# A streaming-encoder block: the gated recurrence before the forgetting attention, its projections in the dense stage

## The chip, the cores and the metric

The kernel runs on one core of a Trainium2 chip. The metric is the device time of one execution in microseconds (us). A core has a matrix engine (TensorE, "PE" in the profile, with its weight loads as "PEld"), VectorE ("DVE"), ScalarE ("ACT"), GpSimd ("POOL"), and queues for transfers, mostly issued by SyncE ("SP") and some by POOL.

## The reference, cut to what matters

The block takes 1024 frames (T) of width 1024. After a normalisation, one input projection feeds three token mixers and their gates; the merged result goes through an output projection and a gated convolutional FFN.

```python
h = _rmsnorm(x, norm_mix_g)
z = h @ w_in
(hq, hf, hi, hg, fq, fk, fv, ff, mq, gate_logits) = jnp.split(z, pts, axis=-1)
y_a = _hgrn2_mixer(hq, hf, hi, hg, ...)   # 4 heads, state 128x128
y_b = _fox_mixer(fq, fk, fv, ff, ...)     # 8 heads x 64, causal
y_c = _memory_mixer(mq, mem_kv, ...)      # 4 heads x 128, 256 memory tokens
gates = jax.nn.sigmoid(gate_logits).reshape(B, T, 3, 1024)
merged = (gates[:, :, 0] * (y_a @ w_br_hgrn) + gates[:, :, 1] * (y_b @ w_br_fox)
          + gates[:, :, 2] * (y_c @ w_br_mem))
x = x + merged @ w_out
x = x + _conv_glu_ffn(_rmsnorm(x, norm_ffn_g), ffn_w_up, conv_w, conv_b, ffn_w_down)
```

The recurrence `_hgrn2_mixer` keeps a state S per head: `S_t = diag(f_t) S_{t-1} + (1 - f_t) i_t`, `o_t = S_t q_t`, with `f = lb + (1 - lb) sigmoid(hf)`, `silu(hq)`, and an output normalised and multiplied by `silu(hg)`. The forgetting attention `_fox_mixer` is causal attention with normalised q and k and a bias from cumulated log forget gates.

## The kernel before, in words

**Products.** Nearly every product is made of three matmuls of split operands (`mm3`, L114 to L116): high by high, high by low, low by high. The high half of an operand is a cast, usually on ACT (L120, names with h), the low half a subtraction on DVE (L128, names with l). A *chunk* is 128 output channels for all 1024 frames. Plainly done (`cm_chunk`, channel-major), a chunk is 48 matmuls of 512 columns. Values, queries and keys of the forgetting attention and the values of the recurrence are made *token-major* (`token_major`): a step is 128 frames by 256 channels, 24 matmuls of 256 columns.

**The dense stage** makes chunks in pairs by a scheme of seven block products instead of eight: a pair takes 84 matmuls of 512 columns, not 96. It needs sums of blocks of the operand (names T1 to T4, B21, ...), made once at the start, and sums of weight blocks, loaded as `rw`. The same scheme serves the FFN and the down projection, with their own sums.

**Order.** Before the change:

1. start: norms, the memory's keys and values (weights `gh`/`gl`), two gate chunks as cover;
2. dense stage, 7 pairs: 4 chunks of memory queries, 10 of gates. Gates go to DRAM (`gd`) as tanh;
3. memory attention, woven with `fox_values` and `fox_proj(0)` (token-major);
4. eight heads of forgetting attention, `fox_attn(p, i)`. Heads with i = 0 have the next `fox_proj` beside them, heads with i = 1 three gate chunks; `fox_prep` transposes and splits a pair's q and k; the last two heads have `hgrn_values` beside them, and one gate chunk;
5. the recurrence: `hgrn_prep(0)` alone (three chunks: f, q, g), then `hgrn_mix(h)` for four heads, the first three each woven with `hgrn_prep(h + 1)`, the fourth with six chunks of the projection of branch 1 (`branch(1)`), of which two more are held behind the last recurrence matmul;
6. branches 0 and 2, output projection (operand `mh`/`ml`), FFN, down projection.

**A head of the recurrence** has two halves of 512 frames. Each half starts with matmuls of `kt` and `qq` (L931, into `A`), runs six levels (H = 64, 32, ..., 2), makes the state update (kE, transposed at L990; L995) and the output (L1001, L1003), and is normalised and transposed (L1022) into `ya`. In a level, DVE subtracts (L948, L949), ACT takes the exponential of X (L950), POOL multiplies one half of X (L951) and DVE the other (L952), and PE multiplies (L961 for the two largest levels, L970 for the others); DVE puts the result into A (L972).

**What sets the order of instructions.** Python generators are woven: `weave` steps the one that is least far along by its count of steps. A scheduler then orders each engine's stream by priority and readiness as it models it; `ahead` raises a mixer's priority by 300, `issue_after` adds an order edge that binds on the same engine. PE, ACT, DVE, POOL and SP's transfers each run in the order so fixed, so an instruction that waits holds all behind it on its engine.

## Time and profile before

| what | value |
|---|---|
| median of 3 runs | 1764.36 us (1763.67 to 1765.61) |
| profiled execution | 1764.18 us |
| its span | 1762.4 us |
| busy: PE, DVE, ACT, POOL | 99%, 67%, 45%, 19% |
| DMA | 227.36 MB, mean 129 GB/s |
| memory attention with its cover | about 236 to 324 us |
| forgetting attention | about 324 to 677 us |
| recurrence, first to last matmul | 690 to 917 us |

A group of the profile is one line of code on one engine: busy time, mean duration (ns), idle time of the engine just before, and what released it. In the timeline each row starts with start and duration; matmuls overlap, so their pace is read from start to start. A bracket at the end gives the idle time ahead of the row and its releaser. PEclk is the clock granted to PE as a share of full speed.

### The profile page before, as it was taken

To read this page: it belongs to the slowest core of one execution; us is meant where nothing else is said; L and a number is where in the kernel's file an instruction comes from. 1 tells how busy PE (TensorE), PEld (TensorE's weight loads), DVE (VectorE), ACT (ScalarE), POOL (GpSimd) and SP (SyncE) were. 2 spreads that over 40 slices of the span, in tenths; PEclk is the share of its full clock that TensorE was granted. 3 is DMA by queue.
4 is the path that set the end of the run, shared out by engine and by line. 5 is a ranking of instruction groups with operands and counts; after the bars stand their busy time and mean duration, and the time that the engine had idled before them with its cause. 6 is when DMAs were issued, how large, how long until landed. Compare 5 with 4: busy or idle time off the path is not lost.

```text
span 1762.4 us, 24530 instructions
## 1 busy us (share of the span) xinstructions
PE 1736.2 (99%) x9069; PEld 1471.4 (83%) x9069; DVE 1185.8 (67%) x2181; ACT 786.7 (45%) x1318; POOL 334.7 (19%) x431
## 2 busy tenths in 40 slices
PE   8999999999999999999989999999999999999998
PEld 6778899989898997888878888788888888778887
DVE  7656445665756567778866755797777877674654
ACT  8633356545555554445331233543343443433332
POOL 1100032443424333334230000111111111100000
PEclk9999999999999999999999999999999999999999
DMA  9533232221212211001226452466454445494772
GB/s 361 178 119 105 83 128 73 76 95 60 91 47 85 84 46 52 25 31 56 77 78 216 153 200 80 136 188 163 139 160 133 119 128 152 144 362 145 238 269 84
DMA packets 83209, 227.36 MB, mean 129 GB/s; under 512 B 9600, under 2 KB 12424, under 8 KB 83088
## 3 DMA queue, kind: packets, MB, share of 16 engines
q1 hardware_dynamic: 65040, 161.29, 26.1%
q0 software_dynamic: 18048, 64.50, 12.6%
q8 instruction: 71, 1.16, 0.3%
q14 instruction: 50, 0.41, 0.1%
HBM read 180.88 MB, written 67.93 MB: 141 GB/s over the span
## 4 chain that ended last, share of the span: by engine, by line
PE 97%; ACT 1%; DVE 1%; DMA 0%; issue 0%; SPq 0%; POOL 0%; DVEq 0%; ACTq 0%
PE pp L115 21%; PE pp L116 21%; PE pp L114 21%; PE lg L115 4%; PE lg L116 4%; PE lg L114 4%; PE tr L114 2%; PE tr L115 2%; PE tr L116 2%; PE lg L970 2%; PE po L836 1%; PE lg L795 1%; PE lg L794 1%; PE po L835 1%; PE po L116 1%; PE po L114 1%
## 5 line engine op out<-in xcount | busy, mean ns | idle before, releaser
L115 PE MATMUL pp<-ul,wh 128*128 128x512 f32 x412 | 165.6, 402 | 0.0
L116 PE MATMUL pp<-uh,wl 128*128 128x512 f32 x412 | 165.4, 401 | 0.0
L114 PE MATMUL pp<-uh,wh 128*128 128x512 f32 x412 | 163.2, 396 | 1.5 <-DVE zt L888 1.5
L115 PE MATMUL pp<-wl,uh 128*128 128x256 f32 (+1 forms) x512 | 145.7, 285 | 0.0
L116 PE MATMUL pp<-wh,ul 128*128 128x256 f32 (+1 forms) x512 | 145.3, 284 | 0.0
L114 PE MATMUL pp<-wh,uh 128*128 128x256 f32 (+1 forms) x512 | 144.7, 284 | 0.0
L120 ACT CAST wh<-s 128x512 fp32r<-128x512 f32 x113 | 68.4, 619 | 152.8 <-PE pp L115 76.8
L120 ACT CAST wh<-raw 128x1024 fp32r<-128x1024 f32 (+2 forms) x76 | 67.5, 890 | 98.9 <-PE pp L115 86.9
L1250 POOL DMA_DIRECT2D rw<-in_w_up x44 | 24.1, 554 | 403.4 <-ACT sqs L1185 169.9
L114 PEld LDWEIGHTS pp<-wh,uh 128*128 128x128 f32 x512 | 96.4, 189 | 1.2
L116 PEld LDWEIGHTS pp<-wh,ul 128*128 128x128 f32 x512 | 96.5, 189 | 0.9
L115 PEld LDWEIGHTS pp<-wl,uh 128*128 128x128 f32 x512 | 96.4, 188 | 0.9
L120 ACT CAST dwh<-wr 128x1024 fp32r<-128x1024 f32 (+1 forms) x42 | 41.1, 980 | 124.6 <-PE tr L115 41.7
L120 ACT CAST wh<-rw 128x512 fp32r<-128x512 f32 x83 | 50.6, 619 | 101.2 <-PE pp L115 59.7
L114 PEld LDWEIGHTS pp<-uh,wh 128*128 128x128 f32 x412 | 78.4, 190 | 17.5 <-DVE zt L888 1.7
L115 PEld LDWEIGHTS pp<-ul,wh 128*128 128x128 f32 x412 | 77.9, 189 | 16.8
L116 PEld LDWEIGHTS pp<-uh,wl 128*128 128x128 f32 x412 | 77.9, 189 | 15.5
L128 DVE TENSOR_TENSOR wl<-raw,wh 128x1024 fp32r<-128x1024 f32 (+2 forms) x76 | 78.4, 1033 | 17.9 <-ACT wh L120 12.7
L128 DVE TENSOR_TENSOR wl<-s,wh 128x512 fp32r<-128x512 f32 x113 | 77.0, 683 | 8.9 <-ACT wh L120 8.9
L128 DVE TENSOR_TENSOR wl<-rw,wh 128x512 fp32r<-128x512 f32 x83 | 55.7, 686 | 29.5 <-PE pp L116 14.1
L951 POOL TENSOR_TENSOR X<-X,kt 128x256 f32<-128x256 f32 x48 | 50.4, 1057 | 124.5 <-ACT X L950 119.5
L128 DVE TENSOR_TENSOR dwl<-wr,dwh 128x1024 fp32r<-128x1024 f32 (+1 forms) x42 | 47.6, 1133 | 39.0 <-ACT dwh L120 39.0
(471 smaller groups left out, 5185.7 us busy)
## 6 DMA issues: line engine op xcount, KB each, us to landing
rw<-in_w_up POOLq DMA_DIRECT2D x44, 512.0 KB, 4.6
sd<-in_w_dn POOLq DMA_DIRECT2D x30, 512.0 KB, 5.9
br<-yd SPq DMA_DIRECT2D x30, 512.0 KB, 5.3
raw<-in_w_cm SPq DMA_DIRECT2D x26, 512.0 KB, 3.4
gd<-gt SPq DMA_DIRECT2D x48, 256.0 KB, 2.0
gt<-gd SPq DMA_DIRECT2D x48, 256.0 KB, 2.8
yd<-fc SPq DMA_DIRECT2D x44, 256.0 KB, 2.5
wr<-sd SPq DMA_DIRECT2D x20, 512.0 KB, 4.4
```

The source lines that it names most:

```text
L114: PE.matmul(ps, lh, rh, start=first, stop=False, skip_group_check=more)
L115: PE.matmul(ps, lh, rl, start=False, stop=False, skip_group_check=more)
L116: PE.matmul(ps, ll, rh, start=False, stop=last, skip_group_check=more)
L120: S.copy(out, in_)
L128: return (sub or V).tensor_sub(l, src, h.bitcast(F32))
L794: PE.matmul(ps[:, :w], qa[i][:, tsl], kh[i][:, s0:s0 + w], start=True, stop=False)
L795: fox_sets[p][3] = PE.matmul(ps[:, :w], qa[i][:, tsl], kl[i][:, s0:s0 + w], start=False, stop=True)
L835: PE.matmul(o, vhl[:, sb, :], ph[:, src], start=(sb == 0), stop=False)
L836: PE.matmul(o, vhl[:, sb, :], pl[:, src], start=False, stop=last)
L951: G.tensor_mul(Xk, Xk, Kv[:, :, 0, :])
L970: PE.matmul(o[:, b * 64:(b + 1) * 64], X[:, b * P:(b + 1) * P], Xq[:, b * bpb:(b + 1) * bpb, :], start=True, stop=True)
L1250: late["raw"] = G.dma_start(raw[:, 2 * i:2 * i + 2, :], src[:, 2 * i:2 * i + 2, :])
```

## The change

The recurrence moves ahead of the forgetting attention, right behind the memory attention. In parts:

- **Dense stage.** All twelve recurrence chunks (q, f, g of four heads) go through it, with the 4 memory queries and 6 gates: 22 chunks, 11 pairs. Their evacuation applies the tanh form there and stores to DRAM (`hd`); `hgrn_load` loads a head's three tiles on SP's queue.
- **Memory attention** is woven with `hgrn_values` (into `Vh`) and two gate chunks.
- **Recurrence.** The four heads are woven with token-major work: `fox_values` (its values go to DRAM, `vfd`), `fox_proj(0)` and `fox_proj(1)` (to DRAM, `zd`), 8 steps a head (9 with the last). `held` ties each such step on PE behind the mixer's matmul three steps back. The normalisation and transposes of a half (`finish`) are issued at the third level of the following half, and its result goes to DRAM (`yad`). At H = 64 and for kE the subtraction goes into the bias of ACT's exponential.
- **Forgetting attention.** `fox_proj(2)` stands alone behind the last recurrence matmul; then eight heads, whose q, k and values come from DRAM, with `fox_proj(3)` beside the first, two gate chunks beside each of the next six, six chunks of `branch(0)` beside the last. Two more chunks are held behind the last PV matmul.
- **After it**, `yc` (memory branch) is loaded on POOL's queue behind the last softmax product, `yb` on SP's; the branches run in the order 0, 2, 1.
- **Smaller.** At the start, the scaling of `xk` tiles (L542) is ordered behind the last cast of x. In the FFN's first units, the casts B21h and T4h are ordered behind the weight casts o5 and o7. The down projection's first block (`down_operands`) is loaded, cast and split within the FFN's last unit.

By the instruction lists, PE has 8661 matmuls instead of 8709: 5760 of 512 columns by 128 instead of 5808, all others alike. DVE has 2211 rows instead of 2178, ACT 1317 instead of 1199, POOL 430 as before, SP 521 transfers instead of 456 (203 of 128x1024 instead of 175, 266 of 128x512 instead of 234).

```diff
-NCOVER, NPAIR = 2, 10
-NFOX = [0, 3, 0, 3, 0, 3, 1]
-_dense = [12, 13, 14, 15] + [16 + 8 * br + j for br, j in ORDER[4:4 + NPAIR]]
+ORDER = [(br, j) for br in (0, 2, 1) for j in range(8)]
+NCOVER, NPAIR, NMEM = 2, 6, 2
+NFOX = [0, 2, 2, 2, 2, 2, 2, 0]
+_dense = [12, 13, 14, 15] + [16 + 8 * br + j for br, j in ORDER[4:4 + NPAIR]] + list(range(12))
...
+            if ch < 12:
+                what, h = divmod(ch, 4)
+                d = t if what == 1 else gate_tile()
+                S.activation(d, t, AF.Tanh, scale=0.5)
+                if what == 1:
+                    V.tensor_scalar(d, d, TMIN, c1[:, h:h + 1], ALU.max, ALU.mult)
+                else:
+                    V.scalar_tensor_tensor(out=d, in0=d, scalar=1.0, in1=t, op0=ALU.add, op1=ALU.mult)
+                SP.dma_start(hd[h, what][:, sl], d)
+                return
...
-                with tc.issue_after(late["square"].ins) if t > 3 else nullcontext():
+                with tc.issue_after(late["square" if t > 3 else "x_cast"].ins):
                     S.activation(xk[t], xk[t], AF.Copy, scale=col(C_GX + t))
...
+    def held(gen, lag=LAG):
+        while True:
+            at = state.get("at", [])
+            with tc.issue_after(at[-lag].ins) if len(at) >= lag else nullcontext():
+                try:
+                    next(gen)
+                except StopIteration:
+                    return
+            yield
...
-    weave((chain(fox_values(), fox_proj(0)), 25), (ahead(memory(), AHEAD), 4 * MEM_STEPS))
+    weave((chain(hgrn_values(), gates_early(NMEM)), 16 + 2 * NMEM), (ahead(memory(), AHEAD), 4 * MEM_STEPS))
...
+        for what, t in ((1, at), (0, qt), (2, gz)):
+            SP.dma_start(t, hd[h, what])
...
+                if H == 64:
+                    nr = ph.tile([P, 4], F32, tag="nr", name="nr", bufs=2)
+                    S.activation(nr, Gv[:, :, 0, H - 1], AF.Copy, scale=-1.0)
+                    for b in range(nb):
+                        S.activation(Xk[:, b, :], Gv[:, b, 0, :], AF.Exp, bias=Gv[:, b, 0, H - 1:H], scale=-1.0)
+                        S.activation(Xq[:, b, :], Gv[:, b, 1, :], AF.Exp, bias=nr[:, b:b + 1])
...
+                if li == 2 and "fin" in state:
+                    state.pop("fin")()
...
-            V.tensor_sub(kE[:, :nb, :], G3[:, :nb, P - 1:P].to_broadcast([P, nb, P]), G3[:, :nb, :])
-            S.activation(kE[:, :nb, :], kE[:, :nb, :], AF.Exp)
+            for b in range(nb):
+                S.activation(kE[:, b, :], G3[:, b, :], AF.Exp, bias=G3[:, b, P - 1:P], scale=-1.0)
...
-    run_all(hgrn_prep(0))
-    for h in range(3):
-        weave((ahead(hgrn_mix(h, ya), AHEAD), HGRN_STEPS), (hgrn_prep(h + 1), 6))
+    open_hgrn()
+    hgrn_load(0)
+    fill = chain(fox_values(), fox_proj(0), fox_proj(1))
+    for h in range(4):
+        weave((ahead(hgrn_mix(h), AHEAD), HGRN_STEPS), (held(islice(fill, 8 + (h == 3))), 8))
+    state.pop("fin")()
+    with tc.issue_after(state["last"].ins):
+        run_all(fox_proj(2))
...
+    for p in range(4):
+        for i in range(2 if p < 3 else 1):
+            if i:
+                fox_prep(p + 1, fox_sets[p][3])
+            count = NFOX[2 * p + i]
+            weave((ahead(fox_attn(p, i), AHEAD), FOX_STEPS),
+                  (held(gates_early(count) if p + i else fox_proj(3)), 2 * count if p + i else 8))
...
+    weave((ahead(fox_attn(3, 1), AHEAD), FOX_STEPS), (held(branch(0, yh, yl, range(6))), 12))
+    with tc.issue_after(late["pv"].ins):
+        run_all(branch(0, yh, yl, (6, 7)))
...
                 if after == "snap":
                     order.enter_context(tc.issue_after(late["split"].ins))
+                    order.enter_context(tc.issue_after(late["o7" if name == "T4" else "o5"].ins))
...
+    def down_operands():
+        raw = pw.tile([P, 4, HB], F32, tag="rw", name="rw", bufs=2)
+        G.dma_start(raw[:, 0:2, :], w_dn[:, 0, 0:2, :])
+        G.dma_start(raw[:, 2:4, :], yd[:, 0, 0:2, :])
+        ops = [operand(raw[:, i, :]) for i in (0, 2, 1, 3)]
+        late["down"] = [Blocks([ops[i + 2 * j][q] for j in range(2)]) for i in range(2) for q in range(2)]
```

How the order moves is seen at three places. The first is PE where the recurrence begins. Before, its first matmuls (L931, from `qq` and `kt`) stood among the matmuls of a chunk of 512 columns (`pp`, a projection):

```order
L114 MATMUL pp<-uh_81,wh 128x512
L115 MATMUL pp<-ul_82,wh 128x512
L116 MATMUL pp<-uh_81,wl 128x512
L114 MATMUL pp<-uh_83,wh 128x512
L115 MATMUL pp<-ul_84,wh 128x512
L931 MATMUL lg<-qq,kt 128x192 x4
L116 MATMUL pp<-uh_83,wl 128x512
L114 MATMUL pp<-uh_85,wh 128x512
L115 MATMUL pp<-ul_86,wh 128x512
```

After the change, the same matmuls (now L951) follow the last matmuls of the memory attention (`po` from `mph`, `mvh`, its values by its probabilities):

```order
L117 MATMUL pp<-uh_85,wl 128x512
L115 MATMUL po<-mph,mvh 128x512
L116 MATMUL po<-mpl,mvh 128x512
L117 MATMUL po<-mph,mvl 128x512
L115 MATMUL po<-mph,mvh 128x512
L116 MATMUL po<-mpl,mvh 128x512
L117 MATMUL po<-mph,mvl 128x512
L951 MATMUL lg<-qq,kt 128x192 x4
L115 MATMUL pp<-wh,uh_71 128x256
L116 MATMUL pp<-wl,uh_71 128x256
L117 MATMUL pp<-wh,ul_72 128x256
```

The last projection chunk of 512 columns now ends ahead of the memory attention's last products, and the token-major fill (256 columns) begins behind the recurrence's first matmuls.

The second place is SP's queue there, after the change. `ychd` and `ycld` store the memory attention's results, `hmf` and `rs` are the recurrence's constants, `ha`, `hq` and `hz` are head 0 (the tiles of `hd`, in two parts), `raw` is a weight of the fill:

```order
L733 DMA ychd<-ych 128x512
L140 DMA raw<-in_w_fqk 128x1024
L733 DMA ycld<-ycl 128x512
L901 DMA hmf<-in_hmask 128x448
L904 DMA rs<-in_mats 128x512
L915 DMA ha_3582<-hd 128x1024
L915 DMA ha_3843<-hd 128x1024
L915 DMA hq_3581<-hd 128x1024
L915 DMA hq_3842<-hd 128x1024
L915 DMA hz_3583<-hd 128x1024
L915 DMA hz_3844<-hd 128x1024
```

Before, `hmf` and `rs` were followed by weights alone, since `ha`, `hq` and `hz` were made on the chip by `hgrn_prep`. The tiles of the constants lie in memory that the memory attention used: `hmf` waits for its last logits, `rs` for the last matmuls but one of the `po` above, and `hq` for the last.

The third place is PE in the last half of the recurrence. Before, from the second level (L961) to the output (L1001, L1003) only the mixer's own matmuls stood there:

```order
L961 MATMUL lg<-X 64x64 x4
L970 MATMUL lg<-X 128x64 x4
L1022 MATMUL tr<-ident,o_9129 128x128
L990 MATMUL tr<-ident,kE 128x128 x3
L970 MATMUL lg<-X 128x64 x4
L1022 MATMUL tr<-ident,o_9129 128x128 x3
L995 MATMUL tr<-Vf,kT 128x128 x3
L970 MATMUL lg<-X 128x64 x4
L1001 MATMUL po<-Vf,A 128x128
L1003 MATMUL po<-St,qe 128x128
```

After the change (L961 is L990, L970 is L1001, L990 is L1024, L1022 is L1058), 38 fill matmuls stand between the second level and the next; these rows are the last of them and what follows:

```order
L115 MATMUL pp<-wh,uh_81 128x256
L116 MATMUL pp<-wl,uh_81 128x256
L1001 MATMUL lg<-X 128x64 x4
L117 MATMUL pp<-wh,ul_82 128x256
L115 MATMUL pp<-wh,uh_83 128x256
L1058 MATMUL tr<-ident,o_5575 128x128
L1024 MATMUL tr<-ident,kE 128x128
L1058 MATMUL tr<-ident,o_5575 128x128
L1001 MATMUL lg<-X 128x64 x4
L1058 MATMUL tr<-ident,o_5575 128x128 x2
L1024 MATMUL tr<-ident,kE 128x128 x2
L116 MATMUL pp<-wl,uh_83 128x256
```

Behind these rows stand 25 more fill matmuls before L1029 and the next level, and 24 before the output. Every half of the recurrence looks like this now, with 92 to 96 fill matmuls of 256 columns, where most halves had 72 of 512 before.

More of the change, by code (lines that the diff above doesn't have):

```diff
@@ L1092, in branch @@
                 yield
[L1094 to L1100 removed]
+    first_branch()
+    weave((ahead(fox_attn(3, 1), AHEAD), FOX_STEPS), (held(branch(0, yh, yl, range(6))), 12))
+    with tc.issue_after(late["pv"].ins):
+        run_all(branch(0, yh, yl, (6, 7)))
+    pf.release()
+    pq.release()
     py = tc.alloc_tile_pool(name="py", bufs=1, side="right", reuse_waits="tile")
@@ L1243, in sum_of, with unit @@
         return t
-    def unit(src, put, begun=None, before=None, after=None):
+    def unit(src, put, begun=None, before=None, after=None, ahead=None):
         raw = pw.tile([P, 4, HB], F32, tag="rw", name="rw", bufs=2)
```

248 lines of the change are left out of this document (132 added, 116 removed).

## The prediction

> **What bounds the kernel now.** I read the page from its top: busy shares, then the chain of work that ended last, then the busy time and granted clock of chosen stretches.
>
> ```profile
> span 1762.4 us, 24530 instructions
> PE 1736.2 (99%) x9069; PEld 1471.4 (83%) x9069; DVE 1185.8 (67%) x2181; ACT 786.7 (45%) x1318; POOL 334.7 (19%) x431
> PE 97%; ACT 1%; DVE 1%; DMA 0%; issue 0%; SPq 0%; POOL 0%; DVEq 0%; ACTq 0%
> ```
>
> TensorE (PE) is the bound almost everywhere: 1762.4 − 1736.2 leaves only 26.2 us of idle time. So there are two ways to gain: fewer matmul columns, and the few places where PE waits or runs at a lower clock. The stretches show those places (columns: from:to, length, then PE, PEld, DVE, ACT and POOL busy, then PEclk, DMA share, GB/s).
>
> ```profile
> 98.00:195.00 97.00, 97.00 (x420) 78.52 (x419) 50.16 (x80) 36.09 (x64) 4.18 (x8) 1.00 0.28 95
> 324.00:367.00 43.00, 43.00 (x311) 40.41 (x310) 30.14 (x82) 23.93 (x46) 23.10 (x27) 1.00 0.30 95
> 586.00:678.00 92.00, 89.77 (x639) 83.34 (x638) 55.18 (x188) 47.68 (x99) 25.25 (x39) 1.00 0.20 66
> 678.00:700.00 22.00, 21.80 (x92) 17.67 (x92) 18.16 (x34) 11.67 (x17) 12.94 (x9) 0.92 0.16 50
> 690.00:867.00 177.00, 177.00 (x1006) 150.32 (x1006) 147.22 (x292) 79.58 (x137) 67.20 (x61) 1.00 0.13 44
> 891.00:933.00 42.00, 36.48 (x213) 32.26 (x212) 28.68 (x60) 14.86 (x28) 13.78 (x16) 0.92 0.36 128
> 1113.00:1124.00 11.00, 8.40 (x47) 6.93 (x45) 6.18 (x12) 9.42 (x20) 3.28 (x4) 1.00 0.40 143
> 1539.00:1553.00 14.00, 11.82 (x43) 8.98 (x43) 12.53 (x14) 5.24 (x6) 2.14 (x4) 0.88 1.02 373
> ```
>
> Row by row: the steady dense stage, one forgetting-attention head with its cover, the end of that attention, the beginning of the recurrence, its first six halves, its uncovered tail, the entry of the FFN and the entry of the down projection. The dense row gives the price of a matmul of 512 columns: 97.00 / 420 = 0.231 us. In the recurrence PE is full, but DVE is busy 147.22 of 177 us (83%): there the second engine is not far behind.
>
> **The change, part by part.** All sums are against the profiled execution, 1764.18 us (its span plus 1.8), which lies 0.2 below the median shown, 1764.36.
>
> *Fewer matmuls.* The dense stage goes from 7 to 11 pairs of chunks. A pair costs 84 matmuls of 512 columns there and 2 x 48 elsewhere, so 4 x 12 = 48 are gone: 48 x 0.231 = **−11.1 us**. Can the dense stage carry recurrence chunks? A pair there takes 84 x 0.231 = 19.4 us of PE, and DVE is busy 50.16 / 97 of it, 10.0 us. The new evacuations add up to four gate products per pair:
>
> ```profile
> L896 DVE SCALAR_TENSOR_TENSOR hq<-hq,zt 128x512 f32<-128x512 f32 x7 | 5.0, 718 | 1.2 <-ACT hq L890 1.1
> ```
>
> 4 x 0.72 = 2.9 us, so 12.9 of 19.4: hidden by the matmuls of the next pair. The new stores and loads of the DRAM tiles (SP, 28 + 32 more of the two large shapes) lie in stretches with a DMA share of 0.13 to 0.30; I cost them at nothing except at the entry below.
>
> *The uncovered tail.* Before, nothing is left to weave beside the last half of the recurrence. The stretch 891 to 933 shows 42.00 − 36.48 = 5.5 us idle and 42 x 0.08 = 3.4 us lost to a clock of 0.92.
>
> ```profile
> 895.52 0.81 PE L931 MATMUL lg<-qq,kt 128*128 128x192 f32 x4
> ...
> 901.39 1.08 PE L970 MATMUL lg<-X 128*128 128x64 f32 x8
> 907.63 1.97 PE L970 MATMUL lg<-X 128*128 128x64 f32 x8 [4.55 <-POOL X L951]
> ...
> 917.32 0.39 PE L1003 MATMUL po<-St,qe 128*128 128x128 f32 x2
> ```
>
> In the new order that place has 38 fill matmuls of 256 columns (the order of PE above). A head's 192 fill matmuls are worth this much:
>
> ```profile
> 340.16 0.28 PE L114 MATMUL pp<-wh,uh 128*128 128x256 f32 x1
> 340.28 0.28 PE L115 MATMUL pp<-wl,uh 128*128 128x256 f32 x1
> ```
>
> 0.118 us from start to start (0.12 in the rows, 0.1175 as a mean over ten), so 38 give 4.5 us and close the 4.55. I take **−8.9**, the whole of it; what the thinner cover costs elsewhere is a term of its own.
>
> *Attention to recurrence.* The lone first projection after the attention is gone.
>
> ```profile
> 678.20 0.72 PE L114 MATMUL pp<-uh,wh 128*128 128x512 f32 x1 [1.51 <-DVE zt L888]
> ...
> 679.15 0.63 PE L116 MATMUL pp<-uh,wl 128*128 128x512 f32 x1
> ```
>
> The two stretches hold 2.2 + 0.2 us of idle and 22 x 0.08 = 1.8 of clock: **−4.2**. At the new end of the attention, two chunks of branch 0 are held behind the last PV, and the loads of yc and yb get those 2 x 24 x 0.231 = 11 us and the last steps of the attention as cover.
>
> *Start, FFN entry, down entry.*
>
> ```profile
> 23.96 1.14 ACT L542 ACTIVATE xk<-xk,cv 128x1024 f32<-128x1024 f32 x1
> ...
> 26.08 0.51 PE L114 MATMUL po<-uh,gh 128*128 128x512 f32 x1 [1.35 <-ACT gh L120]
> ...
> 27.34 0.50 PE L116 MATMUL po<-uh,gl 128*128 128x512 f32 x1 [0.53 <-DVE gl L128]
> ```
>
> The scaling ahead of the cast gh moves behind the last x cast, so gh is 1.1 us earlier, or more: of 1.35 + 0.53 I take **−1.5**.
>
> ```profile
> 1118.37 2.08 ACT B21h L120 x4
> 1120.45 2.08 ACT T4h L120 x4
> ...
> 1123.10 0.50 PE L114 MATMUL pp<-T3h,wh 128*128 128x512 f32 x1 [2.60 <-ACT wh L120]
> ...
> 1545.40 0.79 PE L115 MATMUL pp<-dbl,dwh 128*128 128x512 f32 x1 [1.53 <-DVE dbl L128]
> ```
>
> The casts B21h and T4h now stand behind the weight casts o5 and o7, 4.2 us of ACT less in front of the waiting wh: **−2.3** of 2.60, the rest for the low half of that weight, which comes next. At the down projection the first block is loaded and split a unit earlier; the stretch loses 2.2 idle + 14 x 0.12 = 3.9, of which I take **−3.4**.
>
> Gains: 11.1 + 8.9 + 4.2 + 1.5 + 2.3 + 3.4 = **31.4 us**.
>
> *New: the entry into the recurrence.* PE now goes straight from the last memory matmuls to the first recurrence matmul, and the fill stands behind that. On SP's queue the loads ha, ha, hq wait in order behind rs, which waits for the last memory matmuls but one. No trace shows this place; the nearest rows are the issue of a DMA and its landing.
>
> ```profile
> 1.17 0.42 SPq L209 DMA_DIRECT2D mt<-in_memT  x1
> ...
> raw<-in_w_cm SPq DMA_DIRECT2D x26, 512.0 KB, 3.4
> ```
>
> Four issues at 0.42, a landing at 3.4, and two elementwise steps of 0.6 (like the 0.7 of L896) make 6.3 us of PE idle; then a clock at half pace, as after 907.63 (1.97 us for what took 1.08) or at 679.15, some 1.7 us. I take **+8**. Below it, +4 if the waits of rs fall early; above, +11 with a landing two microseconds later and a longer slow stretch. The matmul that waits holds the whole fill behind it.
>
> [...] The rows speak against a plain threshold: 1.51 us of idle was followed by half pace at 679.15 (0.63 us for a matmul that takes 0.39 to 0.40 elsewhere), and 2.60 us at 1123.10 was not. [...]
>
> *New: a recurrence with thinner cover.* Two rows give PE's work of the mixer:
>
> ```profile
> L115 PE MATMUL pp<-ul,wh 128*128 128x512 f32 x154 | 62.3, 405 | 0.0
> ...
> L115 PE MATMUL pp<-yl,wh 128*128 128x512 f32 x20 | 8.0, 399 | 0.0
> ```
>
> In 690 to 867 there are 3 x 174 matmuls of 512 columns, 120.6 us; the other 56.4 are three heads' own work, 18.8 a head, 9.4 a half. With 96 fill matmuls (11.3) a half now takes PE 20.7 us, where it took 177 / 6 = 29.5. Can the chain over ACT, POOL, DVE and PE go at that pace? The uncovered half of before, from 895.52 to the last L1003 at 917.32 with its wait and low clock, took about 22.0 us: 8 x (22.0 − 20.7) = 10. The change takes subtractions off DVE (H = 64 and kE) and defers each half's end, so I take **+9**. Ends: 0 if it all overlaps, and +29 if the DVE work of the fill comes on top of 22 us (rival b).
>
> *New: recurrence to attention.* 22.7 us of fox_proj(2) cover the last normalise; then fox_prep(0) has eight transposes and their splits with 24 matmuls beside them: **+2** (0 to 5, by the 1.5 to 2.6 us that such entries cost above). The attention heads keep covers of 22.2 or 22.7 us; a head with 22.7 ran full in 324 to 367, DVE at 30.14 of 43: nothing.
>
> New costs: 8 + 9 + 2 = 19. Sum: 1764.2 − 31.4 + 19 = **1752**.
>
> **The rivals.**
>
> *(a) POOL beside a busy DVE slows the recurrence.* POOL's multiply is the step for which PE waited 4.55 us:
>
> ```profile
> 900.24 0.73 POOL L951 TENSOR_TENSOR X<-X,kt 128x256 f32<-128x256 f32 x1 [4.53 <-ACT X L950]
> 903.33 4.25 POOL L951 TENSOR_TENSOR X<-X,kt 128x256 f32<-128x256 f32 x2 [2.36 <-ACT X L950]
> ...
> L951 POOL TENSOR_TENSOR X<-X,kt 128x256 f32<-128x256 f32 x48 | 50.4, 1057 | 124.5 <-ACT X L950 119.5
> ```
>
> One alone takes 0.73 us, two in the crowded tail 4.25, and the mean is 1.057. The halves get shorter, so DVE gets denser, and each half has six such multiplies in a chain: if each takes 0.4 us more than in my 22 us, half of them on the path, a half takes 23.1: 8 x 1.1 = 9 more, **1761**. For it: the two rows. Against: most multiplies are issued well ahead of their matmuls, as the stretch 690 to 867 without idle shows.
>
> [...]
>
> *(b) Slower: DVE work of the fill stands in the recurrence's chain.* Before, the cover brought few DVE instructions that could not wait; now each projection also brings a sum, a product and weight splits:
>
> ```profile
> L732 DVE TENSOR_TENSOR z<-z,fr 128x1024 f32<-128x1024 f32 x7 | 9.7, 1385 | 0.7 <-POOL fr L133 0.7
> L730 DVE TENSOR_REDUCE fr<-fsq 128x16 f32<-128x1024 f32 x7 | 8.5, 1219 | 1.6 <-ACT fsq L729 1.6
> ```
>
> Two of each, and two weight splits of about 1.0 (the mean of L128 below), are 7.1 us for a head that carries fox_proj, 3.6 a half; the first two heads carry fox_values, with the splits alone, 1.0 a half. If this mean of 2.3 comes on top of the 22.0 us, a half takes 24.3: 8 x 3.6 = 29 instead of 9, **1772**. It decides from the point where 31.4 − 8 − 2 = 21.4 us are used up, 2.7 us a half above PE's 20.7, so at 23.4 us. For it: DVE is nearly the bound by its work alone. These groups of 690 to 897, seven halves, belong to the old cover and leave it:
>
> ```profile
> L128 DVE TENSOR_TENSOR wl<-raw,wh 128x512 fp32r<-128x512 f32 (+1 forms) x17 | 16.3, 957 | 0.3 <-ACT wh L120 0.2
> L888 DVE TENSOR_TENSOR zt<-pp,rx 128x512 f32<-128x512 f32 x20 | 13.7, 683 | 3.0 <-PE pp L116 2.8
> ...
> L896 DVE SCALAR_TENSOR_TENSOR hz<-hz,zt 128x512 f32<-128x512 f32 x8 | 6.8, 846 | 0.1
> ...
> L980 DVE TENSOR_TENSOR kE<-Gt 128x512 f32<-128x512 f32 (+1 forms) x7 | 4.9, 698 | 0.0
> ```
>
> With hq's 5.0 they are 41.8 / 7 = 6.0 a half; L980 is 0.7 more that goes. So 147.22 / 6 = 24.5 becomes 24.5 − 6.0 − 0.7 + 3.6 = 21.4 in the last two heads, less the subtractions of H = 64 and the branch work of that stretch: about PE's 20.7. Against: this is no more than the +9 holds already (21.8 a half), and the fill's work on DVE can wait, since its next step is due a whole block later.
>
> *(c) Everything overlaps.* The recurrence stays at PE's pace (+0), the entry costs +4, the next entry +2: 1764.2 − 31.4 + 6 = **1739**.
>
> *(d) The dense saving does not arrive*, since the four extra evacuations of a pair hold PSUM: then + 11, **1763**. Against it stands DVE at 12.9 of 19.4 us.
>
> **How the numbers follow.** My forecast has 0.52 (1745 to 1758, the entry between +4 and +11 and the recurrence a few us either way). (a) has 0.18, (b) 0.13, (c) 0.13, (d) 0.04. Predicted: **1752**. The range takes in (a), (c) and (d), and the lower part of (b): **1738 to 1769**; what is left out is the rest of (b), about 0.1, and a gain beyond (c), as much. About 0.2%, 3.5 us, is what a measurement of this kernel tells from no change. Faster by more (below 1760.8): the forecast, (c), and somewhat under half of (a), **0.74**; within: the rest of (a), (d), and the lower end of (b), **0.14**; slower (above 1767.9): **0.12**.
>
> **What would show it.** 5760 matmuls of 512 columns instead of 5808 and no idle in the dense stage: the first term. A first recurrence matmul (L951) with 4 to 11 us of idle before it and a DMA hq or ha as releaser: the entry. Starts of the recurrence's halves 21.8 us apart on average: +9; at 20.7, case (c); at 23.1 with idle PE released by POOL X, (a); at 24 or more with DVE over 95% busy, (b). A matmul L1001 without a wait of several us in the last half, no waits of 2.60 for wh after B21h and of 1.53 for dbl: the gains. It would be wrong if the attention heads, with their loads from DRAM and the held cover, showed idle that 324 to 367 does not have, since the sum has nothing for them.

## The result, and the profile after

The changed kernel takes **1810.11 us** (median of 4 runs, 1806.11 to 1810.72), the kernel before 1764.26 us. The ratio is 1.0254 (95% interval 1.0236 to 1.0272): 2.5% slower. The prediction, 1752 with a range of 1738 to 1769, was wrong in size and in sign. All medians, here and below, are of fast runs; one slow execution of e6, of 3522 us, is left out.

The page of the changed kernel: its span, the busy shares, and the chain that ended last.

```profile
span 1808.8 us, 24826 instructions
PE 1748.3 (97%) x9021; PEld 1474.3 (82%) x9021; DVE 1207.3 (67%) x2215; ACT 815.9 (45%) x1436; POOL 312.8 (17%) x431
PE 85%; DVE 6%; DMA 3%; ACT 3%; issue 2%; POOL 1%; SPq 0%; DVEq 0%; ACTq 0%; POOLq 0%
```

PE has 48 matmuls fewer, and yet is busy 12.1 us longer (a busy PE at a lower clock counts in full: at 0.50 the matmuls of 512 columns from 694.35 to 695.63 took 0.63 us each, at 1.00 behind 696.42 they took 0.39 to 0.40); its idle time went from 26.2 to 60.5 us. The chain ran over PE for 97% before and for 85% now. So the time is lost in large part to waits, and to the clock behind them.

Where? The first and last logits of the memory attention, a group of the tile `mkh`, before the change and after it (times are of first and last start):

```profile
L114 PE MATMUL lg<-mkh,mqh x32: 277/282/366, 236.1 to 307.3; 128*128 128x256 f32 x32
```

```profile
L115 PE MATMUL lg<-mkh,mqh x32: 276/283/365, 315.3 to 386.1; 128*128 128x256 f32 x32
```

Up to that point the changed kernel is 79.2 us later: four more dense pairs at 19.4 (77.6), and little else. From there to the last matmul of the last mixer (the recurrence's L1003 before, at 917.3; the PV matmul now, at 969.3) it takes 654 us where 681 were needed: 27 us less. But eight chunks of 48 matmuls, 8 x 11.1 = 89 us of PE's work, left that stretch (twelve of the recurrence out, four of gates in). **89 us of cover went out and only 27 came back as time.** Behind the mixers 5.6 us are saved. 79.2 − 27 − 5.6 is the 46 us.

The stretches of the changed kernel that answer to those in the prediction (columns as there):

```profile
28.00:240.00 212.00, 210.75 (x911) 169.90 (x911) 136.82 (x214) 105.88 (x176) 16.07 (x24) 1.00 0.42 144
399.00:421.00 22.00, 7.01 (x34) 6.47 (x33) 12.13 (x21) 13.25 (x26) 4.46 (x5) 0.61 0.67 246
505.00:533.00 28.00, 23.27 (x170) 22.21 (x171) 22.46 (x45) 17.17 (x39) 10.41 (x9) 0.88 0.28 81
627.00:660.00 33.00, 26.31 (x168) 24.14 (x168) 23.19 (x75) 17.41 (x37) 15.88 (x24) 0.84 0.24 79
680.00:700.00 20.00, 14.48 (x60) 11.29 (x59) 16.04 (x46) 10.00 (x19) 12.88 (x16) 0.74 0.12 46
757.00:777.00 20.00, 16.07 (x75) 12.73 (x74) 15.43 (x42) 12.00 (x25) 10.70 (x18) 0.86 0.16 57
839.00:860.00 21.00, 17.07 (x81) 13.86 (x80) 16.22 (x49) 13.48 (x28) 11.35 (x20) 0.84 0.14 44
1165.00:1190.00 25.00, 23.41 (x118) 19.45 (x117) 22.01 (x41) 16.16 (x30) 6.61 (x9) 1.00 0.59 168
1580.00:1605.00 25.00, 25.00 (x110) 20.29 (x109) 20.02 (x24) 12.60 (x15) 4.22 (x8) 1.00 0.74 254
```

In order: the dense stage, full, so that its gain is real; the entry into the recurrence, with 15.0 us idle; the worst half of the recurrence; the beginning of the attention; the three joints of the attention, where the next pair's `fox_prep` runs; the FFN entry and the down entry. Counting idle time and clock together (length minus busy, plus length times the missing share of the clock), the beginning of the attention loses 6.7 + 5.3 = 12.0 us and the joints 10.7 + 6.7 + 7.3 = 24.7. These are upper bounds, since the slow clock counts here also where PE waits: in the first joint the clock was 0.50 from 686.1 to 696.3, and PE was busy 7.11 of these 10.20 us, so 3.6 of the 5.2 us are work that ran slower.

The entry, in PE's timeline and SP's queue of the changed kernel, and the DMA view of 399 to 421 (time from issue to landing at the end):

```profile
399.12 0.40 PE L117 MATMUL po<-mph,mvl 128*128 128x512 f32 x1
414.51 2.90 PE L951 MATMUL lg<-qq,kt 128*128 128x192 f32 x8 [14.99 <-DVE qq L943]
```

```profile
402.17 0.33 SPq L904 DMA_DIRECT2D rs<-in_mats  x1
402.56 1.11 SPq L915 DMA_DIRECT2D ha<-hd  x2
403.77 1.14 SPq L915 DMA_DIRECT2D hq<-hd  x2
```

```profile
hq<-hd SPq DMA_DIRECT2D x2, 512.0 KB, 8.0
```

`hq` is issued 4.3 us after the last memory matmul, since stores, a weight and two constants go ahead, and it lands 8.0 us later, among seven other loads.

One joint in PE's timeline of the changed kernel:

```profile
682.42 0.63 PE L800 MATMUL tr<-ident,zl 128*128 128x128 f32 x4 [0.44 <-issue]
684.17 0.63 PE L800 MATMUL tr<-ident,zl 128*128 128x128 f32 x4 [1.13 <-DVE qa L812]
685.67 0.33 PE L838 MATMUL lg<-kh,qa 128*128 128x128 f32 x1 [0.87 <-DVE st L845]
...
688.81 0.45 PE L869 MATMUL tr<-ident,pt 128*128 128x128 f32 x1 [2.70 <-POOL nfm L833]
...
690.43 0.80 PE L838 MATMUL lg<-kh,qa 128*128 128x512 f32 x1 [0.39 <-DVE st L845]
```

Five waits in eight microseconds with no fill matmul between them. Before the change, 90 fill matmuls of 256 columns (10.6 us) stood around the transposes of one such joint in PE's order; at this one now 24 of 512 columns (5.5 us) stand between the two groups of transposes, and none behind the second group until 693.8.

### The profile page after: what moved, and what is told of

It reads as the page before. It is cut to its first block, busy times and chain, and to the rows that moved or that the text cites. A ratio compares the mean times of both kernels' runs of the same rounds, so it can differ in the third digit from the quotient of the medians.

```text
span 1808.8 us, 24826 instructions
## 1 busy us (share of the span) xinstructions
PE 1748.3 (97%) x9021; PEld 1474.3 (82%) x9021; DVE 1207.3 (67%) x2215; ACT 815.9 (45%) x1436; POOL 312.8 (17%) x431
## 4 chain that ended last, share of the span: by engine, by line
PE 85%; DVE 6%; DMA 3%; ACT 3%; issue 2%; POOL 1%; SPq 0%; DVEq 0%; ACTq 0%; POOLq 0%
PE pp L116 18%; PE pp L117 18%; PE pp L115 18%; PE lg L117 5%; PE lg L115 5%; PE lg L116 5%; PE tr L116 2%; PE tr L115 2%; PE tr L117 2%; PE lg L1001 1%; PE po L882 1%; PE lg L838 1%; PE po L117 1%; PE po L115 1%; PE po L116 1%
## 5 line engine op out<-in xcount | busy, mean ns | idle before, releaser
L121 ACT CAST wh<-s 128x512 fp32r<-128x512 f32 x129 | 77.6, 619 | 174.3 <-PE pp L116 83.8
L117 PE MATMUL pp<-wh,ul 128*128 128x256 f32 (+1 forms) x512 | 148.1, 290 | 0.0
L116 PE MATMUL pp<-wl,uh 128*128 128x256 f32 (+1 forms) x512 | 148.1, 290 | 0.0
L115 PE MATMUL pp<-uh,wh 128*128 128x512 f32 x300 | 122.1, 407 | 0.0
L117 PE MATMUL pp<-uh,wl 128*128 128x512 f32 x300 | 121.4, 405 | 0.0
L116 PE MATMUL pp<-ul,wh 128*128 128x512 f32 x300 | 120.4, 401 | 0.0
L121 ACT CAST wh<-rw 128x512 fp32r<-128x512 f32 x99 | 60.3, 619 | 112.5 <-PE pp L116 67.4
L129 DVE TENSOR_TENSOR wl<-raw,wh 128x1024 fp32r<-128x1024 f32 (+2 forms) x67 | 71.1, 1062 | 23.3 <-ACT wh L121 22.8
L855 ACT ACTIVATE pt<-pt,st 128x128 f32<-128x128 f32 (+3 forms) x64 | 49.7, 777 | 50.1 <-DVE st L852 34.1
L129 DVE TENSOR_TENSOR dwl<-wr,dwh 128x1024 fp32r<-128x1024 f32 (+1 forms) x41 | 46.3, 1130 | 32.5 <-ACT dwh L121 32.5
L115 PEld LDWEIGHTS pp<-uh,wh 128*128 128x128 f32 x300 | 58.3, 194 | 12.0 <-ACT wh L121 0.3
L117 PEld LDWEIGHTS pp<-uh,wl 128*128 128x128 f32 x300 | 57.4, 191 | 12.3
L116 PEld LDWEIGHTS pp<-ul,wh 128*128 128x128 f32 x300 | 57.6, 192 | 11.4
L129 DVE TENSOR_TENSOR pl<-tr,ph 128x512 fp32r<-128x512 f32 (+1 forms) x80 | 49.9, 633 | 20.4 <-ACT ph L121 19.6
L857 POOL TENSOR_SCALAR pt<-pt,st 128x128 f32<-128x128 f32 (+3 forms) x64 | 48.5, 759 | 81.1 <-DVE st L856 55.1
```

What stands on the lines that cost most here:

```text
L115: PE.matmul(ps, lh, rh, start=first, stop=False, skip_group_check=more)
L116: PE.matmul(ps, lh, rl, start=False, stop=False, skip_group_check=more)
L117: PE.matmul(ps, ll, rh, start=False, stop=last, skip_group_check=more)
L121: return S.copy(out, in_)
L129: return (sub or V).tensor_sub(l, src, h.bitcast(F32))
L855: S.activation(pt[:, :ns], pt[:, :ns], AF.Exp, bias=st[:, 2:3], accum_out=st[:, 3:4])
```

## The experiments

All times are medians; "before" is the kernel before, run on the same chip beside them. Two quantities come from the timelines. The *length* of a head or half is the distance between the first logits matmuls of successive heads, or the first matmuls (L931, now L951) of successive halves; the last head ends at its last PV matmul, the last half at its last L1003 (now L1037). Its *cover* is its number of fill matmuls times 0.231 us (512 columns) or 0.118 us (256).

| | heads of the attention, length (cover) | halves of the recurrence, length (cover) |
|---|---|---|
| before | sum 341.3 (229.9) | 30.7, 31.4, 28.7, 28.7, 27.4, 30.6, 28.0 (18 to 23 each), 21.9 (0) |
| changed | sum 338.3 (186.3) | 20.5, 20.2, 24.2, 20.9, 29.0, 20.8, 21.1, 29.7 (9 to 12, the last 16) |

Length less cover is what the eight heads themselves take on PE, with their waits and the slow clock: 111.4 us before, 152.0 after. Those 41 us are most of the miss. The stretches of the eight heads, before and after, say what they are:

```profile
335.10:676.50 341.40, 340.47 (x2278) 310.84 (x2276) 213.24 (x644) 178.98 (x351) 122.93 (x167) 1.00 0.20 68
```

```profile
631.00:969.30 338.30, 317.34 (x1744) 270.09 (x1744) 212.20 (x654) 163.65 (x325) 114.77 (x173) 0.95 0.31 104
```

PE was idle for 0.9 us before and 21.0 after, and the clock went from 1.00 to 0.95, which is worth up to 17.

The changed kernel's own runs lie between 1806.1 and 1810.7 us, so a run that differs from its median by less than some 4 us says little by its time.

**Without the edge held at the attention (e1).**

```diff
-                  (held(gates_early(count) if p + i else fox_proj(3)), 2 * count if p + i else 8))
+                  (gates_early(count) if p + i else fox_proj(3), 2 * count if p + i else 8))
```

> The changed kernel without the edge that ties the cover of the attention heads behind the mixer (held is left out in the loop over the heads; the last head keeps it). Theory: the three joints where fox_prep(p + 1) runs (680 to 700, 757 to 777, 839 to 860 of the changed kernel: 5.5, 3.9 and 3.9 us idle, and a clock of 0.74, 0.86 and 0.84) are bare because the edge keeps the next gates away. Then some 20 us go (16 to 28): 1782 to 1794. Rival: the heads are bound by their own chain over ACT, DVE and POOL with the thinner cover; then the waits only move and the time stays within 5 us of 1810.

1811.5 us (before 1766.9): the rival's time. But its profile shows more than the rival said:

```profile
680.00:700.00 20.00, 20.00 (x101) 16.71 (x100) 12.05 (x31) 10.91 (x20) 10.14 (x16) 1.00 0.19 69
820.00:840.00 20.00, 19.84 (x108) 16.50 (x106) 9.44 (x32) 8.93 (x18) 4.29 (x7) 1.00 0.50 169
840.00:860.00 20.00, 14.71 (x72) 11.63 (x72) 17.66 (x55) 12.42 (x25) 7.20 (x10) 0.74 0.35 117
860.00:880.00 20.00, 12.18 (x58) 9.60 (x57) 13.15 (x38) 10.97 (x24) 10.87 (x18) 0.70 0.15 52
880.00:900.00 20.00, 16.98 (x82) 13.61 (x82) 13.31 (x55) 10.93 (x24) 7.95 (x13) 0.76 0.11 37
```

PE is full through the first joint and until 838, so the joints can be covered. Then the gates are used up, and two heads run bare: 32.7 and 21.8 us, 27.3 on average, for some 13.9 us (111.4 / 8) of PE's own work. The wait moved to where the cover had run out. My theory of the edge fell; what replaced it is that cover is short. Up to there the four heads from 633.8 to 823.1, which load their q, k and v from DRAM like all others, take some 52 us beside their cover, and the first four of before take 51: while cover lasts, those loads cost nothing.

**One gate chunk moved to the entry (e2).** The chunk is taken from beside the memory attention and tied behind that attention's last matmul, ahead of the recurrence.

```diff
+    with tc.issue_after(late["mem"].ins), tc.high_priority(2 * AHEAD):
+        run_all(gates_early(1))
```

> The changed kernel with one of the two gate chunks that lie beside the memory attention put between it and the recurrence on PE (48 matmuls, 11.1 us, ahead of L951). Theory: the 15.2 us of idle at the entry are latency of the loads of ha and hq behind the last memory matmuls, so 11 us of it are covered, and some of the 6 us lost to the clock: 1794 to 1800. Rival: the memory attention needs that chunk itself and loses what the entry gains: 1806 to 1812.

1801.7 us, 8.4 less than the changed kernel, a little short of the theory. What is left of the wait:

```profile
409.84 2.58 PE L951 MATMUL lg<-qq,kt 128*128 128x192 f32 x7 [3.79 <-DVE qq L943]
```

3.8 us instead of 15.0, with 11.1 us of cover put in: the latency is real, and cover hides it one for one.

**The forget gates out of the recurrence (e3), and the recurrence without held (e4).** In e3 the end of `fox_values` is issued behind the last recurrence matmul on PE and the last exponential qe on ACT. In e4:

```diff
-        weave((ahead(hgrn_mix(h), AHEAD), HGRN_STEPS), (held(islice(fill, 8 + (h == 3))), 8))
+        weave((ahead(hgrn_mix(h), AHEAD), HGRN_STEPS), (islice(fill, 8 + (h == 3)), 8))
```

> The changed kernel with the end of fox_values (Abs, Sigmoid, Ln of the forget gates, their transposes and the two scans negF) moved behind the recurrence, beside fox_proj(2). Theory: this end, with its table loads on ACT (1.28 us each) and scans on DVE, stands in the recurrence's chain in the half from 505 to 533, which is 7 us longer than its neighbours: 5 to 9 us go, 1801 to 1805. Rival: that half is long because of the head boundary or the order of the fill: within 3 us of 1810.

> The changed kernel without the edge held for the fill of the recurrence. Theory: the halves take 23.3 us on average because ACT, DVE and POOL form a chain at that pace, so the edge does not matter: within 5 us of 1810. Rival: as at the joints of the attention, the edge keeps the cover from the places that wait: 8 to 16 us go, 1794 to 1802.

e3: 1806.9 us, 3.2 less, between the theory's range and the rival's, and within the spread of the changed kernel's own runs. The long half shrank from 29.0 to 23.6 us as the theory said, but the next two grew from 20.8 and 21.1 to 23.8 and 26.1; the whole recurrence took 185.7 us against 186.4, and its first matmul starts at 412.8 instead of 414.5, so 1.7 us of the gain lie ahead of what was edited. e4: 1811.3 us, the recurrence 185.8. There the fill ran ahead, and the last two halves had almost none: 18.4 and 23.9 us. So another order of the fill did not change the sum.

But the reason that I gave for e4, a chain over ACT, DVE and POOL that goes at 23.3 us a half, does not fit the changed kernel's own profile. Of its eight halves, the second, the fifth and the last:

```profile
435.00:455.20 20.20, 20.20 (x176) 19.80 (x175) 14.88 (x34) 11.26 (x24) 7.64 (x9) 1.00 0.17 54
500.30:529.30 29.00, 23.93 (x174) 22.48 (x173) 21.75 (x45) 19.16 (x46) 12.13 (x11) 0.88 0.21 65
571.20:600.90 29.70, 29.57 (x252) 28.79 (x252) 21.00 (x44) 10.85 (x22) 9.57 (x9) 1.00 0.14 54
```

The second half, and likewise those of 20.9, 20.8 and 21.1 us, ran at PE's pace without a wait, so the chain can go at 20 to 21 us with 11 us of fill. The fifth, in which the end of `fox_values` stands, waited for 5.1 us at a clock of 0.88. The last is long because 16 us of fill and the end of the mixer's work lie in it; PE is full there.

**The small edits alone (e5), and thin cover in the old order (e6).** e5 is the kernel before with three edits: the xk scaling behind the last x cast, B21h and T4h behind o5 and o7, and `down_operands`. e6 is the kernel before with

```diff
-NCOVER, NPAIR = 2, 10
-NFOX = [0, 3, 0, 3, 0, 3, 1]
+NCOVER, NPAIR = 2, 14
+NFOX = [0, 2, 0, 2, 0, 2, 0]
```

> The kernel before with three small edits of the change alone: the xk scaling behind the last x cast, B21h and T4h behind the weight casts o5 and o7, the down projection's first block prepared within the FFN's last unit. Theory: their gains in the changed kernel's trace, 1.3 at the start, 1.0 at the FFN entry and 4.4 at the down entry, are their own: 1764.3 - 6.7 = 1757.5, within 1.5. Rival: they belong to the new order around them (small constants earlier, branches in another order) and are under 3 us here.

> The kernel before with four gate chunks moved from beside the attention heads into the dense stage (9 pairs instead of 7; heads with i = 1 get two gate chunks instead of three, the last pair none), so that a pair of heads has 45 us of cover, as in the changed kernel, and the order is that of before. 24 matmuls of 512 columns fewer. Theory that cover is what the change lacks: the attention loses more than the 5.5 us saved, 1768 to 1790. Rival, that the edge held and the joints of the changed kernel are what costs: nothing is lost, 1757 to 1761.

e5: **1759.2 us** (before 1765.3; ratio 0.9963, 0.9949 to 0.9978), a version that beats both kernels. Both entries run full in its profile:

```profile
1105.00:1130.00 25.00, 25.00 (x127) 21.04 (x126) 17.59 (x31) 15.99 (x31) 5.81 (x8) 1.00 0.34 118
1530.00:1560.00 30.00, 30.00 (x132) 24.39 (x131) 23.35 (x28) 14.37 (x19) 4.93 (x10) 1.00 0.89 312
```

e6: 1781.6 us, 16 more than before, with 24 matmuls fewer (−5.5). This run decides most: nothing is moved but four gate chunks, from beside the attention into the dense stage. Length less cover of the heads: 320.4 − 185.6 = 134.8 us against 111.4, so 23 us are lost where nothing of the new order is in play. Its last heads show it:

```profile
600.00:620.00 20.00, 17.08 (x126) 14.94 (x124) 15.19 (x46) 10.52 (x20) 9.06 (x12) 1.00 0.24 84
620.00:640.00 20.00, 16.88 (x100) 15.33 (x101) 12.73 (x52) 11.79 (x28) 10.49 (x16) 0.83 0.06 16
680.00:700.00 20.00, 14.90 (x77) 12.59 (x77) 10.16 (x30) 7.85 (x15) 3.21 (x4) 0.83 0.06 14
```

**Dealing the same cover out in other ways (e7, e8).** e7 keeps held only for the heads with i = 0; e8 has `NFOX = [0, 3, 1, 3, 1, 3, 1, 0]`.

> The changed kernel with held only for the heads with i = 0; the gates of the heads behind fox_prep (i = 1) may run ahead. If the waits at the joints come from where the cover lies, its two chunks fill the joint and the head still has the rest: 10 to 20 us go, 1790 to 1800. If the attention lacks cover as a whole, the wait moves to the end of these heads: within 5 us of 1810.

> The changed kernel with the twelve gate chunks beside the heads dealt out 3 and 1 (three to the heads behind fox_prep, one to the others) instead of 2 and 2; held stays. If only the place matters: some of the 26 us at the joints go, 1797 to 1805. If held bares the joints whatever the count, since it lets a step go only when the mixer has made one: 1805 to 1815.

e7: 1811.4 us; e8: 1821.6 us, more than even its rival said. In e7 the joint is full and the head behind it is not:

```profile
757.00:777.00 20.00, 20.00 (x101) 16.74 (x100) 12.05 (x26) 10.01 (x17) 8.56 (x14) 1.00 0.30 99
780.00:800.00 20.00, 16.02 (x84) 13.09 (x82) 13.26 (x50) 11.22 (x24) 7.89 (x11) 0.83 0.23 77
```

A pair of heads took 82.4 us in the changed kernel (745.0 to 827.4) and 82.9 here (743.0 to 825.9).

**Giving the cover back (e9, e10).** e9 has `NPAIR` 2 instead of 6 and `NFOX = [0, 3, 3, 3, 2, 3, 2, 0]`; e10 has that without held at the attention.

> The changed kernel with four gate chunks taken back from the dense stage (9 pairs instead of 11) and put beside the attention heads (3, 3, 3, 2, 3, 2 instead of 2 each), held as before; 24 matmuls of 512 columns more (5.5 us). If cover as a whole is what the attention lacks, the idle and slow-clock time from 630 to 940 of the changed kernel (some 34 us) falls by more than 5.5 us and the time is 1792 to 1806. If held keeps the cover from the joints whatever there is, the time goes up by the 5.5 us or more: 1813 to 1820.

> The same as e9_cover_back, and without held at the attention heads. The first run without held (e1_fox_free) ran full for five heads and then had two and a half heads with no cover. With 44 us more cover, theory: the full stretch reaches one and a half heads further and the bare one shrinks, 1790 to 1800. If the heads are bound by their own chain, 1810 to 1818.

1795.3 and 1795.8 us: 15 us *less* than the changed kernel with 24 matmuls *more*, with held or without it. Both as the theory had it. But the amount of cover is not all. Beside the heads of e9 stand 230.5 us of it and beside those of e10 226.2, about as much as before (229.9), and yet length less cover is 139.1 and 139.3 us, 28 more than the 111.4 of before. In e9 the longest waits are at the beginning (4.3 us idle in 585 to 605, at a clock of 0.83) and behind the first joint (2.6 us in 660 to 680, 0.83). In e10 PE is full through the first five heads, and the waits come behind, where the cover is spent:

```profile
589.90:826.00 236.10, 236.10 (x1303) 202.86 (x1302) 139.62 (x406) 111.53 (x213) 75.09 (x105) 1.00 0.28 94
826.00:898.20 72.20, 59.52 (x309) 48.10 (x308) 49.21 (x157) 37.77 (x76) 27.59 (x41) 0.88 0.32 105
```

So both how much cover there is and where it lies count.

**More cover in the recurrence (e11).** `fox_proj(2)` goes into the recurrence's fill (41 steps, 10 or 11 a head).

> The changed kernel with fox_proj(2) woven into the recurrence (41 steps, 10 or 11 a head, instead of 33) instead of alone behind it, and fox_proj(3) beside the first attention head without held. PE's work of a half becomes 9.4 + 14.5 = 23.9 us. Theory that the halves wait for lack of cover: they take 24 to 25 us (mean), no longer than PE's work, against 23.3 for 20.7 in the changed kernel; recurrence and fox_proj(2) together take 192 to 200 instead of 212, less what the first attention head loses without fox_proj(2) before it (5 to 12): 1798 to 1808. Rival: ACT, DVE and POOL carry the same 2.6 us a half in any case, 26.5 a half: 1810 to 1820.

1807.1 us, within the theory's range, but not by its mechanism: the fill did not spread. The first seven halves took 157 us with 10 to 13 us of cover each, the last 40.9 with 26.1, and the beginning of the attention waited longer. It tells little.

**Cover for the last half of the kernel before (e12, e15).** Both carry the three small edits. e12 puts `held` around the six chunks of branch 1; e15 weaves four of them and ties two behind the last half's first matmul:

```diff
-    weave((ahead(hgrn_mix(3, ya), AHEAD), HGRN_STEPS), (branch(1, yh, yl, range(6)), 12))
+    weave((ahead(hgrn_mix(3, ya), AHEAD), HGRN_STEPS), (branch(1, yh, yl, range(4)), 8))
+    with tc.issue_after(state["half"].ins):
+        run_all(branch(1, yh, yl, (4, 5)))
```

> The kernel before with the three small edits of e5_small_alone, and the six chunks of branch 1 beside the last recurrence head held behind the mixer's matmul three steps back, so that they spread over both halves (before, all of them stood in the first). Cover of the last two halves: some 16 us each instead of 19 and 0. Theory: the 5.5 us of idle and 3.4 us of clock of the last half mostly go, and 0 to 2 us come back in the half before: 1750 to 1755. Rival: both halves wait now, 1757 to 1762.

> The kernel before with the three small edits, and two of the six chunks of branch 1 tied behind the first matmul of the last half of the recurrence, so that the last two halves have some 8 and 11 us of cover instead of 19 and 0. If idle time falls faster than cover (none at 18 us a half, 2.6 at 11, 5 to 9 at 0): 1754 to 1757, against 1759.2 for the small edits alone. If idle time just moves with the cover: 1758 to 1762.

e12: 1763.2 us, worse than the small edits alone; its cover did not spread as meant, for the last three halves had 5.8, 11.1 and 22.2 us of it (before, 20.1, 18.9 and 0). e15: 1758.6, the same as the small edits. In e15 the last two halves take 22.4 and 28.0 us, in e5 28.0 and 22.0. Idle time moved with the cover:

```profile
860.00:890.00 30.00, 26.63 (x157) 23.20 (x156) 24.38 (x56) 9.53 (x22) 8.92 (x9) 0.93 0.34 107
890.00:920.00 30.00, 28.84 (x173) 25.15 (x172) 21.07 (x47) 7.82 (x18) 5.73 (x7) 0.95 0.18 53
```

**All remedies together (e13), and with the cover of before (e14).** e13 joins e2, e3 and e9; e14 also has `NPAIR = 0` and three gate chunks beside each of six heads.

> The changed kernel with the edits of e2_entry_cover (8.5 us), e3_forget_late (3.2 us) and e9_cover_back (14.9 us) together. If they are separate costs they add: 1783.5, within 3. If they are one cost seen at three places (the same lack of cover), less than 20 us of the 26.6 go: over 1790.

> As e13_three_together, with two gate chunks more out of the dense stage (8 pairs; three gate chunks beside each of six heads), 12 matmuls of 512 columns more than that, 12 fewer than before the change. If lack of cover is what remains, the attention runs nearly full as before: 1768 to 1778. If the order itself costs (joints under held, the loads of q, k, v, the recurrence with 11 us a half): 1782 to 1788, no better than e13.

e13: 1789.0 us; 21 of the 26.6 us add up, between the two theories. e14: 1790.5 us, no better, and a little above its rival's range. Its attention has 247 us of cover, more than before, and still needs 133 us beside it (380.3 − 247) where before needed 111. So the new order, or the way in which it deals its cover out, costs something of its own:

```profile
330.00:360.00 30.00, 24.54 (x119) 20.81 (x118) 18.56 (x32) 19.28 (x38) 7.02 (x9) 0.85 0.54 198
562.00:587.00 25.00, 21.63 (x130) 19.85 (x131) 18.09 (x66) 14.08 (x29) 14.88 (x20) 0.81 0.08 29
637.00:660.00 23.00, 20.39 (x100) 16.93 (x100) 10.45 (x42) 10.10 (x24) 6.78 (x11) 0.85 0.11 42
739.00:760.00 21.00, 19.80 (x107) 16.49 (x108) 11.25 (x40) 9.28 (x20) 5.25 (x9) 1.00 0.24 79
```

The entry into the recurrence still loses 5.5 + 4.5 us here, the beginning of the attention 3.4 + 4.8, the first joint 2.6 + 3.5, the second 1.2; and the recurrence takes 180.7 us for 8 x 20.7 = 166.

## Why the prediction was wrong, point by point

- **Matmuls, −11.1: right.** The dense stage runs full (210.75 of 212 us). But I booked it by itself. A chunk that moves into the dense stage leaves a mixer without its cover, and only what PE then does not wait is a gain.
- **Start −1.5, FFN entry −2.3, down entry −3.4: right in sum**, though the FFN entry gave 1.0 of its 2.3. Idle at the start fell by 1.6 (PE busy 19.75 of 28 us before, 21.38 in the same stretch after); at the FFN entry 1.6 are left of 2.6; the down entry is full and its 3.9 are gone. e5 shows them alone: 6.1 us.
- **Tail −8.9, attention to recurrence −4.2: won at their places.** The last half runs full (29.57 of 29.70 us), and behind the last attention head there is no wait above 0.3 us until the FFN entry. But the cover that fills them was taken from other places, and the terms below pay for it. e12 and e15 show the same in the old order: the tail's wait appears where cover is short, and moves with it.
- **Entry +8: it was 15.0 idle and some 3 of clock.** The mechanism was right (e2), the size not. The 1.7 us of clock in the sum were my estimate; before, 3.37 us of busy PE went at 0.50 in 907.6 to 911, and here 6.49 us at 0.59 in 414.5 to 421, which is 2.7 lost. I took a landing of 3.4 us from the median of the weight loads; here eight loads were issued within five microseconds and a ninth behind them, hq took 8.0, and more stood ahead in the queue than I counted. (The slow clock falls into the first half of the recurrence and is counted there.)
- **Recurrence +9: it was 21** (186.4 us against 165.6). The price came from the bare half's 22.0 us, taken as the pace of a chain. But that half holds 5.5 us of idle time, a slow clock and the end of the mixer's work, and four halves of the changed kernel went at 20.2 to 21.1 us with PE full. What the 21 are: 7.3 idle (PE busy 179.1 of 186.4 us), some 6 of slow clock, 2.7 of them behind the entry, and some 7 of the mixer's own work that 9.4 us a half leaves out. The kernel before has 4 of these 7: its halves take 227.4 us, of which 139.5 are cover, 5.5 idle and some 3 clock, so 79 and not 8 x 9.4 = 75. The largest wait is the end of `fox_values` in the fifth half; e3 takes it out there, and other halves then wait. Rivals (a) and (b) were about this term, and their signs are not there: POOL's multiply took 0.98 us on average (1.06 before) and PE's longest waits were ended by DVE, and DVE was busy 148.1 of the 186.4 us, 79%. Nor do the two rows of (a) show that a busy DVE makes POOL's multiply longer: DVE was busy for all of the 0.73 us of the one at 900.24 and for 4.19 of the 4.25 us of the two from 903.33. This term did not decide.
- **The attention, +2: it was 41. This is the step that failed.** The heads themselves stood in the sum at nothing, since I wrote that a head with 22.7 us of cover ran full in 324 to 367. The groups of that stretch of the kernel before say otherwise:

```profile
L114 PE MATMUL pp<-wh,uh 128*128 128x256 f32 x64 | 18.2, 284 | 0.0
...
L115 PE MATMUL pp<-ul,wh 128*128 128x512 f32 x16 | 6.4, 398 | 0.0
```

  3 x 64 matmuls of 256 columns are 22.7 us, but 3 x 16 of 512 columns, 11.1 us, ran there too: 33.8 us of cover in 43. That row says nothing about 22. Heads of before had 28.7 us on average (229.9 / 8); in the changed kernel the seven heads ahead of the last have 20.8. The old order at a thinner cover (185.6 us in all) loses 23 us (e6), the new one at 186.3 loses 41 (152.0 − 111.4); the other 17 lie with the order, at the beginning of the attention and the joints (17 by e6, 22 by e14, 28 by e9 and e10). I had named "idle that 324 to 367 does not have" as what would make me wrong, but gave it no price.
- **By sum:** 1752 + 7 (entry) + 12 (recurrence) + 39 (attention) + 1 (FFN entry) = 1811, against 1810.1.
- **The slower rival** had the right sign and the wrong place: it put the loss into DVE's work in the recurrence; it lay in cover that the attention lacked, with DVE busy 16.04 of 20 us in 680 to 700, waiting and waited for.

What stays open: why the new order loses 17 to 28 us that the amount of cover does not explain. The loads of q, k and v from DRAM are not the cause by themselves, for the first heads of e1 and e10 run full with them. The place of the cover is the likely one: with held the joints are bare, without it the last heads are, and no run of the new order deals its cover out as the kernel before did. The change also altered that weave in two ways that no run isolates: the late start of the gates (`FOX_LATE`) is gone, and a head counts 22 steps (`FOX_STEPS`) instead of 28.

## What to carry to other kernels

A latency-bound stage woven with dense work has two budgets: PE's work, and the stage's own chain with the waits that the fill must cover. Work moved out of the weave is only a gain as long as the fill that is left still covers those waits; here 89 us moved out bought 27. Before forecasting, count the fill per head or step, kind by kind, in a stretch that runs full, and in the thinnest that does not; see that it lies where the waits are; and try the thinner fill alone in the old order (e6 needed two lines).

## What the runs showed of the hardware

The clock fell behind several short waits as it did within a long one. In the wait of 14.99 us at the entry it was 1.00 from 399.5 to 402, and 0.50 from 402.8 to 419.8. In 680 to 700 the five waits shown above are 0.4 to 2.7 us each, and the clock was 0.50 from 686.1 to 696.3; it fell when only the first three of them, 0.44, 1.13 and 0.87 us, had passed. PE was busy 7.1 of those 10.2 us, so some 3.6 us of clock stand beside 5.5 us of idle. In the kernel before, one wait of 2.60 us at 1123 cost no clock (1.00 from 1120 to 1130). A 512 KB load that lands in 3.4 us at the median (the 26 weights `raw` of before) took 8.0 us (both loads of hq) and 7.1 us (the median of hz) among nine loads issued in 8.3 us, with the DMA engines busy for 0.67 of the stretch 399 to 421.
